# Expert 0 of a routed expert layer takes 64 token slots in place of 128, and the experts run in another order

## The chip, the cores and the metric

The kernel runs on one core of one Trainium2 chip. The metric is the device time of one execution in microseconds (us), as the median of the runs. TensorE (PE) multiplies matrices, VectorE (DVE) and ScalarE (ACT) do elementwise work, and the sequencer of SyncE (SP) issues all the loads of weights.

## The reference, cut to what matters

Layer 0 is a mixture of a state-space scan and retention with a dense feed-forward; layer 1 is differential attention with a routed expert layer behind it. The change touches only that last layer, which works on 256 tokens of width 1024:

```python
def moe(h, w_router, w_gate, w_up, w_down):
    logits = (h @ w_router).astype(jnp.float32)
    top_val, top_idx = lax.top_k(logits, TOP_K)          # 2 of 8
    top_w = jax.nn.softmax(top_val, axis=-1)
    combine = jnp.sum(jax.nn.one_hot(top_idx, N_EXPERTS, dtype=jnp.float32) * top_w[..., None], axis=-2)
    out = jnp.zeros_like(h)
    for e in range(N_EXPERTS):
        out = out + combine[..., e:e + 1].astype(h.dtype) * swiglu(h, w_gate[e], w_up[e], w_down[e])
    return out
```

`swiglu(h, g, u, d)` is `(silu(h @ g) * (h @ u)) @ d`, with 3584 hidden features in each expert, in 32-bit floats. The 256 tokens choose 512 experts in all, 64 for each expert in the mean. Worked out with the reference on its own inputs, experts 0 to 7 get 60, 52, 39, 90, 48, 47, 107 and 69 tokens.

## The kernel before, in words

Each expert's weights are read once, as 42 loads of two units of 128 x 1024 (1024 KB, here called a pair): 28 pairs of gate and up weights (`exp_gu`), then 14 of down weights (`exp_d`). A pair goes to half of a room named `wide`, or, two pairs in ten, to two tiles named `raw` of 512 KB each. Ten pairs find room at a time, besides five more that are loaded ahead of the layer into memory that the attention has left (`raw2`, L1380). A load waits in SP's queue until its room has been read; all loads stand in one queue in their order.

There are two ways to run an expert.

- Wide, 128 token slots (`expert`, L1480): each unit of weights is split by ACT (L183) and DVE (L184) into a high and a low part (`wsplit`), and each product is three matmuls of 512 columns (`mm3`, L194 to L196).
- Narrow, 64 token slots (`expert_half`, L1413): the weights are multiplied as they are, in 32-bit floats, with two products side by side in the two halves of the array (L1446 for gate and up, L1460 for down).

In both, the tokens of the next expert are gathered (`gather`, L1357 on PE) between the gate-up part and the down part, and the results are scattered back to the tokens at the end (L1525 and L1526, or L1473).

Expert 0 always is itself (`ORDER` starts with it, and its number is a constant), so that its weights can be loaded before the routing is known. The other seven places are filled by count: `sorted` ranks the experts, so place 1 holds the expert with most tokens, and place 7 that with fewest. The place's expert number is a value in memory, `self.ids`, which SP reads into a register (L1245, `TENSOR_LOAD`) before it can issue that place's loads. Places 0 to 3 are wide, places 4 to 7 narrow, in the order wide and narrow in turn: 0, 7, 1, 6, 2, 5, 3, 4. Below, W0 is the wide expert at place 0, N7 the narrow one at place 7, and so on.

If an expert has more tokens than slots, a general path behind the eight experts runs it again for the rest (L1251 to L1265). It is skipped when none has more. The Tile framework orders each engine's instructions by its own estimate; a block `issue_after(x)` makes its instructions stand behind `x` in their engine's queue, without a wait.

Of the kernel before, what the change touches and what calls it, by code (L numbers as in the profile page):

```python
# [19 lines left out]
P = 128  # L20
# [5 lines left out]
NE = 8  # L26
CAP = P
HALF = 64

ORDER = (0, 7, 1, 6, 2, 5, 3, 4)  # L30
SLOTS = (CAP,) * 4 + (HALF,) * 4
FE = 3584
LAM_INIT = 0.8 - 0.6 * math.exp(-0.3)

# [105 lines left out]
class Net:  # L140
# [18 lines left out]
    def mm(self, i):  # L159
        return self.pp.tile([P, 512], F32, name=f"mm{i}", tag=f"mm{i}", bufs=1)  # L160
# [12 lines left out]

    def wraw(self, ap):
        t = self.pw.tile([P, 1024], F32, name="raw", tag="raw", bufs=5)
        self.nc.sync.dma_start(t, ap)
        return t

    def wsplit(self, raw):
# [274 lines left out]
    def run(self):  # L454
        self.start()
        self.layer0()
        self.layer1()
        self.experts()
# [704 lines left out]
class Layer1Experts(Layer1):  # L1163
# [72 lines left out]
    def experts(self):  # L1236
        nc = self.nc
        v = nc.vector
        self.nraw, self.wide, self.al_slot, self.rest_slot = -5, (2, 3, 0, 1), 4, 4
        self.place, self.eid, self.rooms = self.rank, [0] * NE, {}  # L1240
        g = self.gather(0, 0)
        self.sorted()
        for i, n in enumerate(ORDER):
            if n:
                self.eid[n] = nc.values_load(self.ids[0:1, n:n + 1], engines=[mybir.EngineType.SP],  # L1245
                                             min_val=0, max_val=NE - 1)
            nxt = ORDER[i + 1] if i + 1 < NE else None
            run = self.expert if SLOTS[n] == CAP else self.expert_half
            g = run(n, g, 0, nxt, not i, nxt is None)

        more = nc.values_load(self.more[0:1, 0:1], min_val=0, max_val=256)  # L1251
        with self.tc.If(more > 0):
            self.nraw, self.wide, self.al_slot, self.rooms = 0, (3, 0, 1), 2, {}
            for t in range(2):
                v.memset(self.moe[:, t, :], 0.0)
            for n in range(NE):
                extra = nc.values_load(self.extra[0:1, n:n + 1], min_val=-P, max_val=256)
                with self.tc.If(extra > 0):
                    self.expert(n, self.gather(n, SLOTS[n]), SLOTS[n], None, False, False)
            for t in range(2):  # L1260
                for j in range(2):
                    c = slice(512 * j, 512 * j + 512)
                    u = self.scr("s3")
                    v.tensor_tensor(u, self.moe[:, t, c], self.rest[:, 2, c], op=ALU.mult)
                    self.put(t, c, u)  # L1265

    def sorted(self):

        nc = self.nc
        v = nc.vector  # L1270
        room = self.pc.tile([P, 384], F32, name="order", tag="dt_ex")
        at = [0]

        def new(shape):
            n = math.prod(shape)
            at[0] += n
            r = room[:, at[0] - n:at[0]]
            return r.rearrange("p (a b) -> p a b", b=shape[1]) if len(shape) == 2 else r

        e8 = lambda ap: ap[:, None, :].to_broadcast([P, NE, NE])  # L1280
        io = self.con[:, C_IO:C_IO + NE]
        pn = self.tr()
        for t in range(2):
            nc.tensor.matmul(pn[:, 0:NE], self.con[:, C_ONE:C_ONE + P], self.sel[:, t, :], start=t == 0, stop=t == 1)
        cnt, key, pos = (new([NE]) for _ in range(3))
        v.tensor_copy(cnt, pn[:, 0:NE])
        v.tensor_copy(key, pn[:, 0:NE])
        v.tensor_scalar(key[:, 0:1], key[:, 0:1], 1024.0, None, op0=ALU.add)
        cmp = self.scr("s3", (P, 2, NE, NE))
        mine, other = key[:, :, None].to_broadcast([P, NE, NE]), e8(key)  # L1290
        v.tensor_tensor(cmp[:, 0], other, mine, op=ALU.is_equal)
        v.tensor_tensor(cmp[:, 1], other, mine, op=ALU.is_gt)
        v.tensor_tensor(cmp[:, 0], cmp[:, 0], self.con[:, C_TIE:C_TIE + NE * NE].rearrange("p (a b) -> p a b", b=NE),
                        op=ALU.mult)
        v.tensor_reduce(pos, cmp.rearrange("p i a b -> p a i b"), axis=AX.XY, op=ALU.add)
        v.tensor_scalar(pos, pos, 1.0, None, op0=ALU.add)

        hot = new([NE, NE])
        v.tensor_tensor(hot, e8(pos), io[:, :, None].to_broadcast([P, NE, NE]), op=ALU.is_equal)
        self.place, self.wts = (new([2, NE]) for _ in range(2))  # L1300
        num = new([2, NE])
        u = self.scr("s3", (P, 2, NE, NE))
        for src, dst in ((self.rank, self.place), (self.cw, self.wts)):
            v.tensor_tensor(u, src[:, :, None, :].to_broadcast([P, 2, NE, NE]),
                            hot[:, None].to_broadcast([P, 2, NE, NE]), op=ALU.mult)
            v.tensor_reduce(dst, u, axis=AX.X, op=ALU.add)
        v.tensor_tensor(u[:, 0], e8(io), hot, op=ALU.mult)
        v.tensor_tensor(u[:, 1], e8(cnt), hot, op=ALU.mult)
        v.tensor_reduce(num, u, axis=AX.X, op=ALU.add)
        v.tensor_scalar(num[:, 0], num[:, 0], -1.0, None, op0=ALU.add)  # L1310
        self.ids = new([NE]).bitcast(I32)
        v.tensor_copy(self.ids, num[:, 0])
        for lo, hi, cap in ((0, 4, CAP), (4, NE, HALF)):
            v.tensor_scalar(num[:, 1, lo:hi], num[:, 1, lo:hi], -float(cap), None, op0=ALU.add)
        self.extra = new([NE]).bitcast(I32)
        v.tensor_copy(self.extra, num[:, 1])
        top = new([1])
        v.tensor_reduce(top, num[:, 1], axis=AX.X, op=ALU.max)
        v.tensor_scalar(top, top, 0.0, None, op0=ALU.max)
        self.more = new([1]).bitcast(I32)  # L1320
        v.tensor_copy(self.more, top)
# [7 lines left out]
    def gather(self, n, base):  # L1329
# [4 lines left out]
        v = nc.vector  # L1334
        half = SLOTS[n] == HALF and not base
        w = HALF if half else P
# [43 lines left out]
    def raw2(self, ap):  # L1380

        n = self.nraw
        self.nraw += 1

        k = n + 5 if n < 0 else n % (2 + 2 * len(self.wide)) - 2
        if n >= 0 and k < 0:
            return [self.wraw(ap[:, 1024 * i:1024 * i + 1024]) for i in range(2)]
        if n == -1:
            t = self.x[:, 0:2, :]
        else:  # L1390

            key = (k // 2, n < 0)
            if key not in self.rooms:
                self.rooms[key] = self.big(((5, 4) if n < 0 else self.wide)[k // 2], (P, 4, 1024), name="wide")
            t = self.rooms[key][:, 2 * (k % 2):2 * (k % 2) + 2]
        self.nc.sync.dma_start(t.rearrange("p u c -> p (u c)"), ap)
        return [t[:, i] for i in range(2)]

    def weights(self, name, n, *at):
# [13 lines left out]
    def expert_half(self, n, gathered, base, nxt, first, final):  # L1413

        nc = self.nc
        v = nc.vector
# [6 lines left out]
        ap = self.big(5, (P, FE // P, HALF), name="ef")  # L1423
# [7 lines left out]
        t = None  # L1431
        for b in range(FE // 512):
# [3 lines left out]
            for u in range(0, KD, 2):  # L1436
# [4 lines left out]
                for i in range(2):  # L1441
                    k = u + i
                    for g in range(2):
                        for h, s in enumerate(sides):
                            c = 512 * g + 256 * h
# [4 lines left out]
            t = self.scr("s3", (P, 256))  # L1450
# [18 lines left out]
        for t in range(2):  # L1469
            for j, s in enumerate(sides):  # L1470
                c = slice(512 * j, 512 * j + 512)
                pt = self.tr()
                mm(pt, pT[s, P * t:P * t + P], y[s], start=True, stop=True)  # L1473
                if final:
                    self.put(t, c, pt)
                else:
                    v.tensor_tensor(self.moe[:, t, c], self.moe[:, t, c], pt, op=ALU.add)
        return out

    def expert(self, n, gathered, base, nxt, first, final):  # L1480
# [27 lines left out]
        for u in range(0, nd, 2):  # L1508
            raw = self.raw2(self.weights("exp_d", n, u // 2))
            w = [self.wsplit(r) for r in raw]  # L1510
            steps = [(f, j) for f in (u, u + 1) for j in range(2)]
            for f, j in sorted(steps, key=lambda s: s[1]) if u == nd - 2 else steps:
                hi, lo = w[f - u]
                c = slice(512 * j, 512 * j + 512)
                self.mm3(py[j], ah[:, f, :], al[:, f, :], hi[:, c], lo[:, c], f == 0, f == nd - 1)
# [36 lines left out]
```

## Time and profile before

| | us |
|---|---|
| median of 3 runs | 2021.04 |
| lowest and highest run | 2015.29, 2026.21 |
| the profiled execution's own time | 2024.08 |
| span of its profile, first to last instruction | 2021.8 |
| PE busy in it | 1950.6 |

The span is 2.3 us shorter than its own execution. The expert layer takes the last 900 us of it. Times in the profile count from the start of the span.

### The profile page before, as it was taken

How to read it: one execution, taken by the hardware profiler on the slowest of the kernel's cores; microseconds unless marked ns; L12 is line 12 of the kernel's file. 1: busy time of each engine (PE TensorE's matmuls, PEld its weight loads, DVE VectorE, ACT ScalarE, POOL GpSimd, SP SyncE). 2: the span in 40 equal slices, each digit the busy share in tenths (PEclk: the TensorE clock that was granted, in tenths of full speed). 3: DMA queues.
4: the chain of work that ended last, by engine and by line, in shares of the span. 5: the costliest groups of instructions: out<-in, count | busy, mean ns of one | idle time of the engine just before them, and what ended most of it. 6: DMA issues, size and time to landing. Idle time of an engine off the chain costs nothing.

```text
span 2021.8 us, 26680 instructions
## 1 busy us (share of the span) xinstructions
PE 1950.6 (96%) x9894; PEld 1444.9 (71%) x9894; DVE 1226.4 (61%) x2105; ACT 906.1 (45%) x1373; POOL 10.1 (1%) x12
## 2 busy tenths in 40 slices
PE   7999999999999999999989999989999999999996
PEld 4776778777888888877857887648863786558762
DVE  5568578745877565577666886049811984059710
ACT  5535356533423212245365775138712773148610
POOL 0000000000000000000000000000000000000010
PEclk9999999999999999999999999999999999989999
DMA  8323434442655555424325499999999999999897
GB/s 319 114 94 105 145 112 150 136 141 64 207 181 174 174 174 167 155 94 116 114 105 219 166 344 337 418 418 417 369 390 418 417 379 362 417 418 390 341 376 312
DMA packets 103865, 502.68 MB, mean 249 GB/s; under 512 B 13104, under 2 KB 13744, under 8 KB 69296
## 3 DMA queue, kind: packets, MB, share of 16 engines
q1 hardware_dynamic: 103728, 500.91, 66.2%
q8 instruction: 79, 1.29, 0.3%
q14 instruction: 58, 0.48, 0.1%
HBM read 495.62 MB, written 5.24 MB: 248 GB/s over the span
## 4 chain that ended last, share of the span: by engine, by line
PE 81%; DMA 9%; DVE 6%; ACT 3%; issue 1%; SPq 0%; ACTq 0%; DVEq 0%
PE mm L196 17%; PE mm L195 17%; PE mm L194 17%; PE mm L1446 8%; DMA wide<-exp_d 3%; PE acc L195 2%; PE acc L196 2%; PE acc L194 2%; DMA wide<-exp_gu 2%; DVE lo L184 2%; DMA raw<-exp_d 2%; PE acc L1460 2%; PE tr L1357 1%; PE acc L315 1%; PE tr L1473 1%
## 5 line engine op out<-in xcount | busy, mean ns | idle before, releaser
L183 ACT ACTIVATE hi<-raw 128x1024 fp32r<-128x1024 f32 x224 | 237.3, 1060 | 411.5 <-PE mm L196 204.8
L184 DVE TENSOR_TENSOR lo<-raw,hi 128x1024 fp32r<-128x1024 f32 x224 | 273.0, 1222 | 177.1 <-ACT hi L183 169.9
L184 DVE TENSOR_TENSOR lo<-wide,hi 128x1024 fp32r<-128x1024 f32 x268 | 324.7, 1223 | 37.0 <-ACT hi L183 16.7
L183 ACT ACTIVATE hi<-wide 128x1024 fp32r<-128x1024 f32 x268 | 282.2, 1061 | 77.7 <-PE mm L196 52.2
L195 PE MATMUL mm<-lo,q 128*128 128x512 f32 x448 | 178.9, 399 | 2.1 <-DVE lo L184 2.0
L196 PE MATMUL mm<-hi,q 128*128 128x512 f32 x448 | 176.8, 395 | 0.0
L194 PE MATMUL mm<-hi,hh 128*128 128x512 f32 x416 | 169.0, 407 | 1.7 <-DVE b L856 1.3
L1446 PE MATMUL mm<-wide,q 128*64 128x256 f32 x1424 | 168.3, 382 | 0.0
L195 PE MATMUL mm<-lo,hh 128*128 128x512 f32 x416 | 165.2, 397 | 0.0
L196 PE MATMUL mm<-hi,hl 128*128 128x512 f32 x416 | 164.7, 398 | 0.0
L194 PE MATMUL mm<-hi,q 128*128 128x512 f32 x448 | 159.6, 397 | 0.0
L194 PE MATMUL mm<-h2h,hi 128*128 128x512 f32 (+1 forms) x376 | 142.5, 379 | 1.3 <-ACT hi L183 1.3
L195 PE MATMUL mm<-h2l,hi 128*128 128x512 f32 (+1 forms) x376 | 141.9, 377 | 0.0
L196 PE MATMUL mm<-h2h,lo 128*128 128x512 f32 (+1 forms) x376 | 141.7, 378 | 0.0
L1446 PEld LDWEIGHTS mm<-wide,q 128*64 128x64 f32 x1424 | 100.4, 137 | 55.8 <-issue 8.6
L1451 DVE TENSOR_TENSOR s<-s,mm 128x256 f32<-128x256 f32 x28 | 11.8, 421 | 192.7 <-ACT s L1449 192.7
L1460 PE MATMUL acc<-wide,ef 128*64 128x512 f32 x360 | 88.2, 601 | 18.6 <-DMA wide<-exp_d 18.6
L195 PEld LDWEIGHTS mm<-lo,q 128*128 128x128 f32 x448 | 85.4, 191 | 25.5 <-DVE lo L184 4.7
L194 PEld LDWEIGHTS mm<-hi,q 128*128 128x128 f32 x448 | 85.0, 190 | 22.8 <-ACT hi L183 3.0
L194 PEld LDWEIGHTS mm<-hi,hh 128*128 128x128 f32 x416 | 78.9, 190 | 27.9 <-issue 8.9
L196 PEld LDWEIGHTS mm<-hi,q 128*128 128x128 f32 x448 | 85.4, 191 | 18.5 <-issue 1.5
L196 PEld LDWEIGHTS mm<-hi,hl 128*128 128x128 f32 x416 | 78.7, 190 | 17.0 <-issue 0.8
(393 smaller groups left out, 3327.8 us busy)
## 6 DMA issues: line engine op xcount, KB each, us to landing
wide<-exp_gu SPq DMA_DIRECT2D x177, 1024.0 KB, 10.6
wide<-exp_d SPq DMA_DIRECT2D x91, 1024.0 KB, 11.8
raw<-exp_gu SPq DMA_DIRECT2D x92, 512.0 KB, 10.9
raw<-odd_wmod SPq DMA_DIRECT2D x48, 512.0 KB, 4.3
raw<-w_in SPq DMA_DIRECT2D x44, 512.0 KB, 3.7
raw<-ffn_gu SPq DMA_DIRECT2D x44, 512.0 KB, 4.4
raw<-exp_d SPq DMA_DIRECT2D x42, 512.0 KB, 15.0
raw<-even_wmod SPq DMA_DIRECT2D x36, 512.0 KB, 3.7
```

What stands on the lines that cost most here:

```text
L183: nc.scalar.activation(hi, raw, AF.Copy)
L184: nc.vector.tensor_tensor(lo, raw, hi.bitcast(F32), op=ALU.subtract)
L194: mm(ps, lh, rh, start=first, stop=False, skip_group_check=skip)
L195: mm(ps, lh, rl, start=False, stop=False, skip_group_check=skip)
L196: mm(ps, ll, rh, start=False, stop=last, skip_group_check=skip)
L315: nc.tensor.matmul(ps[r:r + 32, :], self.cond[:, k, :], raw[:, 512 * kk:512 * kk + 512], start=k < 4, stop=k >= 4)
L1357: nc.tensor.matmul(pt[:, w * kk:w * kk + w], self.x[:, 2 + t, P * (k + kk):P * (k + kk) + P], pn[:, t, 0:w], start=t == 0, stop=t == 1)
L1446: behind = mm(ps[s, 256 * g:256 * g + 256], xg[:, k, :], raw[i][:, c:c + 256], start=k + g == 0, stop=k == KD - 1, skip_group_check=True)
L1451: v.tensor_tensor(t, sg, ps[:, 256:512], op=ALU.mult)
L1460: mm(py[s], ap[:, f, :], raw[f - u][:, 512 * j:512 * j + 512], start=f == 0, stop=f == nd - 1, skip_group_check=True)
L1473: mm(pt, pT[s, P * t:P * t + P], y[s], start=True, stop=True)
```

## The change

Places 0 and 4 to 7 are narrow now, 1 to 3 wide. The order is 0, 1, 7, 2, 6, 3, 5, 4: N0, W1, N7, W2, N6, W3, N5, N4. The narrow function learns to write the sum of the outputs as the first expert. The general path gets a second pass for place 0, since expert 0 can have up to 256 tokens, and 64 + 128 don't hold them. SP's read of a place's expert number is placed behind the last load of the expert before it.

```diff
-ORDER = (0, 7, 1, 6, 2, 5, 3, 4)
-SLOTS = (CAP,) * 4 + (HALF,) * 4
+ORDER = (0, 1, 7, 2, 6, 3, 5, 4)
+SLOTS = (HALF,) + (CAP,) * 3 + (HALF,) * 4
...
     def wraw(self, ap):
         t = self.pw.tile([P, 1024], F32, name="raw", tag="raw", bufs=5)
-        self.nc.sync.dma_start(t, ap)
+        self.loaded = self.nc.sync.dma_start(t, ap)
         return t
...
             if n:
-                self.eid[n] = nc.values_load(self.ids[0:1, n:n + 1], engines=[mybir.EngineType.SP],
-                                             min_val=0, max_val=NE - 1)
+                with self.tc.issue_after(self.loaded.ins):
+                    self.eid[n] = nc.values_load(self.ids[0:1, n:n + 1], engines=[mybir.EngineType.SP],
+                                                 min_val=0, max_val=NE - 1)
...
                 with self.tc.If(extra > 0):
                     self.expert(n, self.gather(n, SLOTS[n]), SLOTS[n], None, False, False)
+                if not n:
+                    with self.tc.If(extra > P):
+                        self.expert(n, self.gather(n, SLOTS[n] + P), SLOTS[n] + P, None, False, False)
...
-        for lo, hi, cap in ((0, 4, CAP), (4, NE, HALF)):
+        for lo, hi, cap in ((0, 1, HALF), (1, 4, CAP), (4, NE, HALF)):
             v.tensor_scalar(num[:, 1, lo:hi], num[:, 1, lo:hi], -float(cap), None, op0=ALU.add)
...
-        self.nc.sync.dma_start(t.rearrange("p u c -> p (u c)"), ap)
+        self.loaded = self.nc.sync.dma_start(t.rearrange("p u c -> p (u c)"), ap)
...
                 if final:
                     self.put(t, c, pt)
+                elif first:
+                    v.tensor_copy(self.moe[:, t, c], pt)
                 else:
                     v.tensor_tensor(self.moe[:, t, c], self.moe[:, t, c], pt, op=ALU.add)
```

## Rows read from the trace of the kernel before

**Rows 1.** The page's second part: the span in 40 slices of 50.5 us; each digit is a busy share in tenths.

```profile
PE   7999999999999999999989999989999999999996
...
DMA  8323434442655555424325499999999999999897
```

**Rows 2.** The busy time of each engine in stretches of 50 us, in which W0 runs and ends, N7 runs and W1 begins. The columns are the stretch, its length, the busy us (and count) of PE, PEld, DVE, ACT and POOL, then the granted clock of TensorE (1.00 is 2.4 GHz, 0.50 is 1.2 GHz), the share of the DMA engines, and GB/s.

```profile
1100.00:1150.00 50.00, 46.90 (x236) 39.92 (x235) 41.01 (x109) 34.48 (x48) 0.00 (x0) 0.90 0.37 136
1150.00:1200.00 50.00, 50.00 (x229) 40.94 (x228) 46.90 (x44) 40.92 (x44) 0.00 (x0) 1.00 0.98 367
1200.00:1250.00 50.00, 50.00 (x246) 39.29 (x244) 38.57 (x37) 33.41 (x40) 0.00 (x0) 1.00 0.86 327
1250.00:1300.00 50.00, 50.00 (x435) 31.62 (x435) 3.98 (x9) 5.58 (x15) 0.00 (x0) 1.00 0.99 394
1300.00:1350.00 50.00, 44.11 (x199) 19.05 (x196) 11.82 (x16) 12.71 (x23) 0.00 (x0) 1.00 1.01 417
```

**Rows 3.** The timeline of PE where the experts meet: start, busy us, line, tile written and tiles read, count, and in brackets the idle time and who ended it. In order: the gather of W0's tokens and W0's first matmul; a narrow gather inside W0; the first matmul of N7; the first row and the last of N7's down part; the first matmul of N4 and the last row of its down part.

```profile
1113.47 6.05 PE L1357 MATMUL tr<-s,x 128*128 128x128 f32 x32
...
1120.38 0.50 PE L194 MATMUL mm<-hi,q 128*128 128x512 f32 x1
...
1204.02 3.68 PE L1357 MATMUL tr<-s,x 128*128 128x64 f32 x32
...
1245.38 0.65 PE L1446 MATMUL mm<-wide,q 128*64 128x256 f32 x2
...
1305.68 1.93 PE L1460 MATMUL acc<-wide,ef 128*64 128x512 f32 x6
...
1335.88 1.94 PE L1460 MATMUL acc<-wide,ef 128*64 128x512 f32 x8 [0.47 <-DMA wide<-exp_d]
...
1917.23 0.65 PE L1446 MATMUL mm<-wide,q 128*64 128x256 f32 x2
...
2008.83 1.92 PE L1460 MATMUL acc<-raw,ef 128*64 128x512 f32 x8
```

**Rows 4.** The same timeline inside N7: two pairs of its gate-up part with parts of the next gather between them, a stretch of its down part, and the first of seven gaps in a row that end with a load (the last of them is the row at 1335.88 in rows 3).

```profile
1298.52 1.95 PE L1446 MATMUL mm<-wide,q 128*64 128x256 f32 x16
1300.39 1.60 PE L1357 MATMUL tr<-s,x 128*128 128x128 f32 x12
1301.93 1.95 PE L1446 MATMUL mm<-wide,q 128*64 128x256 f32 x16
1303.81 1.38 PE L1357 MATMUL tr<-s,x 128*128 128x128 f32 x10
...
1307.91 7.51 PE L1460 MATMUL acc<-wide,ef 128*64 128x512 f32 x33
...
1320.91 1.94 PE L1460 MATMUL acc<-wide,ef 128*64 128x512 f32 x8 [1.40 <-DMA wide<-exp_d]
```

**Rows 5.** The timeline of SP's queue: all loads of expert weights up to the first that had to wait for W0 to read its room (`wide` and `x` 1024 KB each, `raw` 512 KB).

```profile
886.84 0.33 SPq L1396 DMA_DIRECT2D x<-exp_gu  x1
...
1014.27 0.80 SPq L1396 DMA_DIRECT2D wide<-exp_gu  x2
...
1018.67 64.14 SPq L1396 DMA_DIRECT2D wide<-exp_gu  x6
1085.03 7.13 SPq L176 DMA_DIRECT2D raw<-exp_gu  x3
1092.25 0.38 SPq L1396 DMA_DIRECT2D wide<-exp_gu  x1
1094.57 0.33 SPq L176 DMA_DIRECT2D raw<-exp_gu  x1
1094.95 0.42 SPq L1396 DMA_DIRECT2D wide<-exp_gu  x1
1097.29 0.33 SPq L176 DMA_DIRECT2D raw<-exp_gu  x1
1103.10 0.80 SPq L1396 DMA_DIRECT2D wide<-exp_gu  x2
1136.59 3.12 SPq L176 DMA_DIRECT2D raw<-exp_gu  x3
```

**Rows 6.** The DMA issues in the stretch 1000 to 1110 us: tile and source, count, KB each, median us from issue to landing.

```profile
raw<-exp_gu SPq DMA_DIRECT2D x5, 512.0 KB, 4.9
```

**Rows 7.** SP's reads of the expert numbers: SP's wait on the line that makes them (us in total, times, longest), and the read itself (shortest, median and longest ns, first and last start).

```profile
SPq L1245 <- DVE order L1312: 31.2, 1, 31.2
...
L1245 SPq TENSOR_LOAD <-order x7: 263/276/468, 1135.1 to 1889.1; - x7
```

**Rows 8.** DVE's timeline: the making of the numbers, and the first tile `raw` of W0 read for its low part.

```profile
1134.93 0.16 DVE L1312 CAST order<-order 128x8 int32<-128x8 f32 x1
1135.00 1.22 DVE L184 TENSOR_TENSOR lo<-raw,hi 128x1024 fp32r<-128x1024 f32 x1
```

**Rows 9.** Busy time by stretches of 20 us, columns as in rows 2: the end of N5, the change to W3, and a stretch of N4's down part.

```profile
1760.00:1780.00 20.00, 16.49 (x72) 5.22 (x70) 0.00 (x0) 0.00 (x0) 0.00 (x0) 1.00 1.02 419
1780.00:1800.00 20.00, 18.43 (x41) 9.36 (x38) 9.84 (x11) 8.10 (x9) 0.00 (x0) 0.66 1.02 416
1980.00:2000.00 20.00, 15.42 (x66) 3.75 (x64) 0.00 (x0) 0.00 (x0) 0.00 (x0) 1.00 1.02 420
```

## The prediction

> **What bounds the kernel now.** I read the page's slices first. PE is busy 9 tenths or more nearly everywhere, and from slice 24 on the DMA engines are too [rows 1]. So the expert layer has two limits close together, and a mean says nothing; I went by stretches. While W0 runs, the DMA share is 0.37, 0.98 and 0.86, and PE is busy 46.9, 50 and 50 of 50 us: W0 is bound by PE. While N7 runs PE is first full and then busy 44 of 50, with the DMA at 417 GB/s: N7 ends bound by its loads [rows 2]. PE's timeline shows that in single instructions: a pair of N7's gate-up part takes PE 1.87 us (1298.52 to 1300.39) [rows 4], and at the end of N7's down part each row waits for a load, from 1320.91 to 1335.88 six steps of 2.495 us [rows 3, 4]. So a pair costs 2.495 us by DMA and 1.87 us by PE in a narrow expert. A wide one can't be faster than its matmuls: W0 took 1245.4 - 1120.4 = 125.0 us for 42 pairs, 2.98 us each [rows 3].
>
> What the reader is to see: a wide expert is slower than its loads, a narrow one faster; a narrow one behind a wide one eats what the wide one's time let the DMA put aside, and then waits.
>
> **The change part by part.**
>
> *W0 becomes N0.* By SP's timeline 15.5 pairs are issued before W0's first matmul (1 + 2 + 6 + 1 + 1 + 2 pairs of `wide` and `x`, five `raw` of half a pair = 2.5) and then nothing until 1136.59 [rows 5], because all room is full. This store is the reason that place 0 can gain what the others can't: it needs only 26.5 of its 42 pairs from the DMA.
>
> N0's start: W0's gather took 6.05 us, a narrow one later took 3.68, at a full clock; W0's first matmul came 0.86 us behind its gather [rows 3]. Between 1113.5 + 3.7 + 0.9 = 1118.1 and 1120.4 I take 1119.6, since the clock in that stretch is below 1 [rows 2].
>
> N0 by PE: 28 pairs x 1.87 = 52.4, and the gather of W1 (12 + 10 of its 32 matmuls took 1.54 + 1.38 us, so 4.2) make 56.6 us [rows 4]. N7 needed 1305.68 - 1245.38 = 60.3 [rows 3], which holds W0's scatter too; N0 has none in front. I take 58. Down: 33 matmuls in 7.51 us, so 112 in 25.5 [rows 4]. End by PE: 1119.6 + 58 + 25.5 = 1203.
>
> N0 by DMA: the next load waits until N0 has read the first tile `raw`, that is five pairs and a half: 1119.6 + 5.5 x 1.87 + 0.4 to issue = 1130.3. The queue is empty then; a half pair landed 4.9 us after its issue [rows 6], of which 1.25 is its transfer, so 3.6 us are latency. 1130.3 + 3.6 + 26.5 x 2.495 = 1200, and 1.9 for the last pair: 1202. The two limits meet, so N0 ends at about 1203, and PE's own work before it doesn't change. W0 ended at 1245.4: **-42 us**. Bounds: 1200 (the DMA with the early start), and 1120.4 + 60.3 + 32.1 (N7's whole down part with its waits, 1305.68 to 1337.8) = 1213; so -45 to -32.
>
> *The six experts between* are N7, W1, N6, W2, N5, W3 before, from N7's first matmul at 1245.38 to N4's at 1917.23, 671.9 us [rows 3]. They are W1, N7, W2, N6, W3, N5 after it. Each wide one still follows a narrow one that ended out of loads, each narrow one a wide one: no change, **0**.
>
> *N4 follows N5 instead of W3.* Before it took 2010.75 - 1917.23 = 93.5 us [rows 3], less than its 42 x 2.495 = 104.8 us of loads, as W3 had let the DMA run ahead. Behind N5 nothing is put aside: 104.8 from N5's last load to its own. **+11**. Bounds: 0, if something is still in store, and a slower TensorE.
>
> That last bound is a matter of the clock. N5's end had PE busy 16.5 of 20 us and the clock at 1.00, N4's down part 15.4 of 20 and 1.00; but at the change from N5 to W3 the mean is 0.66 over 20 us, which is 13.6 us at the lower level, 1.2 GHz [rows 9]. The Trainium skill, "TensorE: Matmul & The Clock Gate", section "HAM oscillation — how this bites in real kernels", says that a matmul loop that waits for a load between bursts falls back to half the clock, again and again. By that rule N4, which will wait at each pair, would run its 60.3 + 25.5 us of PE work at half speed, 172 us, and the sum would be +36 instead of -31. The trace agrees for waits at the change of experts, and disagrees for the short waits of 0.5 us at each pair [rows 4, 9]; by the rows the sum stays.
>
> *The reads of the expert numbers.* SP's wait for them is 31.2 us [rows 7], the largest single thing that the edit to L1245 takes away. It is worth almost nothing in this trace. The numbers are made at 1134.93; the first `raw` that the next load needs is read by DVE at 1135.00 to 1136.22 [rows 8], and that load is issued at 1136.59 [rows 5]. SP stood behind a read, but the room wasn't free either: the cover is the full store. Without the edit the read would have gone bad here, as N0 frees the room at 1130. Now all seven reads stand between two experts' loads; behind each stand the next place's 42 loads, and PE waits for those. The read takes 0.28 us [rows 7], while a load keeps the DMA busy for 2.495 us with more in the queue: **0**; if that cover went, about 1 us each with its register work, 4 that move, so 4 us.
>
> *Small things.* Copying N0's sums instead of adding them and a third `tensor_scalar` in `sorted` lie on engines that are idle in a narrow expert (DVE 4.0, ACT 5.6 of 50 us [rows 2]): 0. What W0's DVE and ACT did (84 units split) is gone, and both were off the path. The second pass for place 0 is code in a skipped branch; expert 0 has 60 tokens, so it isn't run: 0, and at most 1 us for the jump.
>
> **Sum:** -42 + 0 + 11 + 0 = -31 us. The profiled execution took 2024.08 us (its span 2021.8 and 2.3 around it), so 1993; it lies 3 us above the median of the runs, and against the median it is 1990.
>
> **The rivals.**
>
> *More gain.* N4 pays nothing and the 13.6 us at the lower clock don't come back: -42 - 7 = -49 at most, or 1972 to 1980. For it: such a stretch belongs to one change of experts here, and nothing says that it must come again. Against: N4 needs all 42 pairs, and N5 waits for loads at its end [rows 9].
>
> *Less gain.* N0 goes at N7's pace, with waits in its down part, and ends at 1213: -32 + 11 = -21, and with one more stretch at the lower clock at N5's end -14: 2000 to 2010. For it: N0's two limits lie within 2 us of each other, and any waste shows. Against: the store of 15.5 pairs.
>
> *No change.* If the read in the queue held SP until the loads in flight had landed, each of the seven borders would cost a landing of 4.9 us, 34 in all, which eats the sum. For it: reads are now at every border. Against: the last read, at 1889.1 [rows 7], stood before N4's loads already, and a wait of SP's own shows on the first of them alone (31.2 us, once).
>
> *Slower.* N4 at the lower clock: a pair would take 3.74 us by PE, 1.25 more than its load. That takes the gain of 31 away after 25 of N4's pairs, 93 us at half clock; all of N4 gives 2057. For it: the 0.66 of rows 9, and the two levels differ by more than a narrow expert's slack (1.87 against 2.495 us). The Trainium skill's rule above speaks for it as well. Against: the clock stayed at 1.00 through two such stretches.
>
> *The change doesn't do what it says:* were expert 0 over 64 tokens, the general path would run a whole wide expert, 125 us more at least: 2115. Against: 60 tokens by the reference.
>
> **How the numbers follow.** The forecast (1980 to 2000) has 0.60, more gain 0.13, less gain 0.15; these three are faster by over 0.5% (about 10 us, which is what a measurement of this kernel can tell from no change): 0.88. No change 0.07. Slower 0.05, of which the lower clock has 0.03 and the general path 0.02. The time is the forecast's, 1990. The range goes from N0 at its best with a little of the extra gain, 1976, to the less gain's middle, 2005; what lies outside are the last two cases (0.12) and the ends of the gains.
>
> **What would show it.** Right: the first matmul of the wide expert's gate-up near 1205 instead of N7's at 1245; loads issued again at about 1130, with the DMA share near 1 from there to W1's end; 670 to 675 us from N0's end to N5's; each row of N4's gate-up part ending a wait for a load, 105 us in all. Wrong: N0's down part with gaps of 0.5 us from its start, SP's gaps of 5 us around the reads, N4 with a clock below 1, or any matmul behind L1259.

## The result, and the profile after

The changed kernel takes 1994.62 us (median; 1992.13 to 1999.70), the kernel before, run beside it, 2022.17 us. The ratio is 0.9884, with a 95% interval of 0.9858 to 0.9910: faster, by 27.6 us in the medians. The profiled execution took 1992.13 us with a span of 1990.0, 31.8 us under the span of before. One execution among all the runs below, of gather_128_fill, went at a mean clock of 0.556 (3203.83 us) and is left out of every comparison.

The page's second part after, as in [rows 1]:

```profile
PE   6999999999999999999999999999999999999986
...
PEclk9999999999999999999998799999999999999999
DMA  8332434442655455532433499999999999999997
```

Both limits are still close together. What has changed is where the DMA's full part begins, and the stretches of 50 us that answer to [rows 2] show it:

```profile
1100.00:1150.00 50.00, 48.50 (x331) 36.31 (x331) 16.26 (x86) 11.70 (x25) 0.00 (x0) 0.80 0.43 164
1150.00:1200.00 50.00, 50.00 (x362) 27.43 (x360) 3.46 (x8) 7.98 (x21) 0.00 (x0) 1.00 1.02 418
1200.00:1250.00 50.00, 47.38 (x197) 31.76 (x194) 35.58 (x35) 30.59 (x34) 0.00 (x0) 1.00 1.02 418
...
1300.00:1350.00 50.00, 49.64 (x249) 37.25 (x249) 34.13 (x34) 29.96 (x37) 0.00 (x0) 1.00 0.88 331
```

From 1150 to 1250 us the DMA share is 1.02 where it was 0.98 and 0.86, and ACT and DVE are nearly free while N0 runs (8.0 and 3.5 of 50 us). The dip of the DMA share that stood at W0's end (0.86) now stands at W1's end (0.88).

PE's timeline where the experts meet, as in [rows 3]: part of N0's gather, its first matmul, the first and last rows of its down part, the rest of N5's down part, and the last row of N4's.

```profile
1114.28 6.64 PE L1362 MATMUL tr<-s,x 128*128 128x64 f32 x30
...
1121.36 1.12 PE L1451 MATMUL mm<-wide,q 128*64 128x256 f32 x2
...
1181.96 1.93 PE L1465 MATMUL acc<-wide,ef 128*64 128x512 f32 x6
...
1206.97 1.94 PE L1465 MATMUL acc<-wide,ef 128*64 128x512 f32 x8 [0.45 <-DMA wide<-exp_d]
...
1871.57 1.46 PE L1465 MATMUL acc<-wide,ef 128*64 128x512 f32 x6
...
1977.07 1.92 PE L1465 MATMUL acc<-raw,ef 128*64 128x512 f32 x8
```

N0's matmuls end at 1208.9 us (W0's at 1245.2), N5's at 1873.0, N4's at 1979.0. So the first expert gives back 36.3 us, the six between take 664.1 in place of 672.1, and N4 takes 106.0 in place of 93.5: -36.3 - 8.0 + 12.5 = -31.8, which is the difference of the spans.

SP's timeline around the first load that has to wait for N0, as in [rows 5], and below it SP's own wait in that stretch, as in [rows 7]:

```profile
1103.32 0.80 SPq L1401 DMA_DIRECT2D wide<-exp_gu  x2
1135.39 3.45 SPq L176 DMA_DIRECT2D raw<-exp_gu  x4
```

```profile
SPq L1253 <- DVE order L1326: 24.6, 1, 24.6
SPq L176 <- PE mm L1451: 7.6, 4, 5.8
```

The reads of the expert numbers are gone from here, and the read of the branch's value (L1253) has slid into their place. It is over by 1129.5; the load comes 6 us later, and SP's wait on its line (L176, 5.8 us the longest) is for N0's matmuls, so again it is the room that is missing, not SP.

The reads themselves (shortest, median and longest ns, first and last start) now stand at the seven borders:

```profile
L1247 SPq TENSOR_LOAD <-order x7: 264/268/271, 1191.1 to 1852.9; - x7
```

None of them holds SP for the loads in flight. The last one starts at 1852.9, N4's first load goes out at 1853.7 (the chain below), and the load issued just before the read, the last of N5's, lands only at 1871.0.

The chain of work that ended last, from N4's loads on (start, length, what):

```profile
1853.72 19.84 DMA wide<-exp_gu
...
1873.68 15.47 DMA wide<-exp_gu
...
1954.54 20.65 DMA wide<-exp_d
...
1975.33 3.67 PE acc L1465 x16
```

Before, N4's chain began with 26 us of matmuls and reached the loads at 1943; now all of N4 is loads, down to its last two pairs.

### The profile page after: what moved, and what is told of

Read it like the earlier page. It is cut to its first block, busy times and chain, and to the rows that moved or that the text cites. A ratio compares the mean times of both kernels' runs of the same rounds, so it can differ in the third digit from the quotient of the medians.

```text
span 1990.0 us, 26467 instructions
## 1 busy us (share of the span) xinstructions
PE 1909.2 (96%) x9936; PEld 1385.0 (70%) x9936; DVE 1120.0 (56%) x2011; ACT 815.4 (41%) x1286; POOL 10.1 (1%) x12
## 4 chain that ended last, share of the span: by engine, by line
PE 74%; DMA 16%; DVE 6%; ACT 3%; issue 1%; SPq 0%; ACTq 0%; DVEq 0%
PE mm L195 16%; PE mm L196 16%; PE mm L194 16%; PE mm L1451 7%; DMA wide<-exp_d 5%; DMA wide<-exp_gu 5%; DMA raw<-exp_d 3%; PE acc L195 2%; PE acc L196 2%; PE acc L194 2%; DVE lo L184 1%; PE acc L315 1%; PE tr L1362 1%; PE acc L1465 1%; PE tr L1478 1%
## 5 line engine op out<-in xcount | busy, mean ns | idle before, releaser
L184 DVE TENSOR_TENSOR lo<-wide,hi 128x1024 fp32r<-128x1024 f32 x202 | 244.9, 1224 | 22.2 <-ACT hi L183 5.9
L183 ACT ACTIVATE hi<-wide 128x1024 fp32r<-128x1024 f32 x202 | 212.7, 1061 | 52.8 <-PE mm L196 34.0
L1451 PE MATMUL mm<-wide,q 128*64 128x256 f32 x1760 | 212.6, 386 | 8.5 <-DMA wide<-exp_gu 8.4
L1451 PEld LDWEIGHTS mm<-wide,q 128*64 128x64 f32 x1760 | 125.0, 138 | 82.8 <-DMA wide<-exp_gu 14.3
L195 PE MATMUL mm<-lo,q 128*128 128x512 f32 x336 | 133.0, 396 | 1.3 <-DVE lo L184 1.3
L196 PE MATMUL mm<-hi,q 128*128 128x512 f32 x336 | 131.3, 391 | 0.0
L1465 PE MATMUL acc<-wide,ef 128*64 128x512 f32 x456 | 111.7, 600 | 17.0 <-DMA wide<-exp_d 16.9
L194 PE MATMUL mm<-hi,q 128*128 128x512 f32 x336 | 112.9, 392 | 0.0
L194 PEld LDWEIGHTS mm<-hi,hh 128*128 128x128 f32 x416 | 78.2, 188 | 27.6 <-issue 9.7
L1465 PEld LDWEIGHTS acc<-wide,ef 128*64 128x64 f32 x456 | 32.8, 136 | 87.8 <-issue 52.2
L195 PEld LDWEIGHTS mm<-lo,hh 128*128 128x128 f32 x416 | 78.3, 188 | 17.0 <-issue 2.0
L341 DVE SCALAR_TENSOR_TENSOR s<-raw,cond,s 128x512 f32<-128x512 f32 x112 | 80.4, 749 | 1.2
```

What stands on the lines that cost most here:

```text
L183: nc.scalar.activation(hi, raw, AF.Copy)
L184: nc.vector.tensor_tensor(lo, raw, hi.bitcast(F32), op=ALU.subtract)
L194: mm(ps, lh, rh, start=first, stop=False, skip_group_check=skip)
L195: mm(ps, lh, rl, start=False, stop=False, skip_group_check=skip)
L196: mm(ps, ll, rh, start=False, stop=last, skip_group_check=skip)
L341: nc.vector.scalar_tensor_tensor(t, w, self.cond[:, k, i:i + 1], t, op0=ALU.mult, op1=ALU.add)
```

## The experiments

Stage ends read from each run's PE timeline, in us; a stage runs from the end of one expert's last down matmul to the end of the next one's, the first stage from its first matmul. The six are the experts between the first and N4. The fifth column adds up the stretches at 1.2 GHz inside the six, from the granted clock in each trace.

| kernel | first expert | the six | N4 | at 1.2 GHz in the six | span |
|---|---|---|---|---|---|
| before | 124.8 | 672.1 | 93.5 | 17.1 | 2021.8 |
| after | 87.6 | 664.1 | 106.0 | 0 | 1990.0 |
| after_again | 88.3 | 675.7 | 106.0 | 23.9 | 1998.8 |
| after_third | 87.9 | 670.1 | 106.0 | 13.7 | 1993.0 |
| gather_128 | 85.4 | 665.6 | 105.7 | 3.4 | 1984.3 |
| gather_128_again | 85.4 | 670.8 | 105.7 | 13.7 | 1986.6 |

**The changed kernel again: after_again.**

> The changed kernel once more, on the chip of the other three runs of this set, as their base. Every theory expects a ratio of 0.984 to 0.991 to the kernel before, N0's last down matmul near 1209 us, and TensorE's clock at 1.2 GHz from about 1107 to 1128 us.

Measured: ratio 0.9901 (0.9874 to 0.9929); N0's last down matmul ends at 1206.0, the clock is at the lower level from 1104.6 to 1125.0. Its span is 8.8 us longer than that of the first profile: the layer begins 3.6 us earlier (N0's first matmul at 1117.8, there at 1121.4), and the six take 11.6 us more. The stretches of 20 us at two changes from a narrow expert to a wide one show why:

```profile
1205.00:1225.00 20.00, 18.43 (x49) 9.90 (x46) 10.98 (x12) 9.07 (x10) 0.00 (x0) 0.74 1.02 417
1430.00:1450.00 20.00, 19.09 (x44) 9.59 (x41) 9.81 (x11) 7.28 (x9) 0.00 (x0) 0.66 1.02 419
```

In the table, against the first profile of after, 17.1 us at 1.2 GHz (before) go with 8.0 us more in the six, 23.9 (after_again) with 11.6 and 13.7 (after_third) with 6.0: a little under half a microsecond for each.

**The wider gather: gather_128.**

```diff
+        ww = w if n or base else P
...
-            nc.scalar.activation(pn[:, t, 0:w], p[:, t, 0:w], AF.Copy, scale=self.rs2[:, t:t + 1])
+            nc.scalar.activation(pn[:, t, 0:ww], p[:, t, 0:ww], AF.Copy, scale=self.rs2[:, t:t + 1])
...
-        per = 512 // w
+        per = 512 // ww
...
-                    nc.tensor.matmul(pt[:, w * kk:w * kk + w],
+                    nc.tensor.matmul(pt[:, ww * kk:ww * kk + ww],
```

> Only expert 0's gather is changed: its 32 matmuls stream 128 columns (the 64 wanted ones twice), as W0's gather did, and the second copy is not read. Theory (the clock): N0 came 6 us later than forecast because TensorE's clock rose at 1128.0 in place of 1118.0 us, and it rose late because the narrow gather keeps the array less busy than the wide one. Then the clock rises near 1118, the first load behind the store is issued near 1130 in place of 1135.4, N0's down part ends near 1203 in place of 1209, and the time is 4 to 6 us under that of the changed kernel. Rival (N0 is late because its gather starts late, behind the routing, and the clock is an effect of chance): the clock rises at 1124 or later, and the time is within 2 us of the changed kernel, or longer by the 2 us more that wide matmuls cost.

The clock is in the last column but two, over stretches of 4 us. First before, then after, then gather_128:

```profile
1116.00:1120.00 4.00, 3.80 (x26) 3.61 (x25) 1.23 (x3) 1.22 (x3) 0.00 (x0) 0.75 0.00 0
1120.00:1124.00 4.00, 4.00 (x24) 3.46 (x23) 2.59 (x10) 3.10 (x7) 0.00 (x0) 1.00 0.03 6
```

```profile
1120.00:1124.00 4.00, 3.89 (x17) 2.83 (x18) 1.35 (x7) 1.08 (x3) 0.00 (x0) 0.50 0.01 4
1124.00:1128.00 4.00, 4.00 (x22) 2.22 (x20) 3.76 (x22) 2.07 (x5) 0.00 (x0) 0.50 0.00 0
```

```profile
1112.00:1116.00 4.00, 4.00 (x24) 4.00 (x24) 0.50 (x2) 0.41 (x1) 0.00 (x0) 0.60 0.00 0
1116.00:1120.00 4.00, 4.00 (x33) 2.78 (x33) 1.43 (x7) 1.49 (x4) 0.00 (x0) 1.00 0.01 4
```

PE's timeline in gather_128 has the gather and N0's first matmul at

```profile
1111.63 5.06 PE L1363 MATMUL tr<-s,x 128*128 128x128 f32 x28 [1.01 <-ACT s L1355]
1116.62 0.65 PE L1452 MATMUL mm<-wide,q 128*64 128x256 f32 x2
```

and SP's the first load behind the store at

```profile
1128.34 3.45 SPq L176 DMA_DIRECT2D raw<-exp_gu  x4
```

In this run the layer began 2.7 us earlier than in after, so times are counted from the start of the gather's long row (1111.63, in after 1114.28). The clock fell at 1104.9 and rose 10.2 us later; in after it fell at 1107.6 and rose 20.5 us later. The load behind the store was issued 16.7 us behind the gather's start, in after 21.1; N0 ended 90.4 us behind it, at 1202.0, in after 94.6: 4.2 us less. Twice the columns cost next to nothing. In gather_128_again, where the clock rose only at the end of the gather, PE's timeline has it as

```profile
1107.60 6.32 PE L1363 MATMUL tr<-s,x 128*128 128x128 f32 x28 [1.01 <-ACT s L1355]
```

That is 0.226 us for each matmul, against 0.221 us for those of after.

The edit also lets the gathered tokens be copied out in two halves instead of all at once, which the theory doesn't name; but in after PE stood only 0.12 us ahead of N0's first matmul (1121.24 to 1121.36) and nowhere behind it until the waits for loads at N0's end, so that is not the 4 us. The theory stands on the place and the size in the profile. The median was 1987.42 us, 11.1 us under that of after_again; the profiles explain some 4 of them, so the pair was run again.

**The pair again: after_third and gather_128_again.**

> The changed kernel a third time, as the base of the next run. Both theories expect 1992 to 2000 us.

> The kernel with the wider gather again, beside the changed one, on one chip. In the first set it was 11 us faster by the medians, where the clock's earlier rise explains 5. Theory (5 us by the clock's rise; the rest was that the changed kernel had more stretches at 1.2 GHz later by chance): 4 to 7 us faster by the medians, and equal within 2 us where runs of equal mean clock less the first stretch are compared. Rival (the wider gather also keeps off later stretches): 9 to 12 us faster again.

Measured: 1993.40 us (ratio 0.9867) and 1992.66 us (0.9875, 0.9851 to 0.9900), no difference in the medians. The profiles repeat the first set: the clock rises 20.5 us and 10.2 us behind its fall, and N0 ends 95.0 and 91.6 us behind the start of the gather's long row, 3.4 us apart. Both profiles have 13.7 us at 1.2 GHz in the six, and their spans are 6.4 us apart (2.5 of it ahead of the gather); why the medians are not lies in the executions without a trace. Over the nine runs of either kernel in both sets the means are 1995.5 and 1990.6 us, 4.9 apart, with a standard error of some 2 us. Neither expectation is met as it was written. That the wider gather is worth about 4 us is shown by the profiles (all seven with the narrow gather end N0 94.4 to 95.3 us behind the gather's start, these two at 90.4 and 91.6), and not by the medians of these runs.

**More matmuls in PE's waits: gather_128_fill.**

```diff
+            if nxt is not None and SLOTS[nxt] == CAP and u >= nd // 2:
+                if u == nd // 2:
+                    fill = self.mm(3)
+                with self.tc.issue_after(behind.ins):
+                    for _ in range(1 if u < nd - 2 else 3):
+                        mm(fill[:, 0:P], self.ident, self.con[:, 0:P], start=True, stop=True)
```

> The kernel with the wider gather, and in each narrow expert that a wide one follows (N0, N7, N6) nine matmuls of 128 columns more on PE whose result nobody reads: one behind each of the last pairs of the down part, where PE waits for loads, and three behind the last, where it waits for ACT. Theory (the stretches at 1.2 GHz near these three changes, which come and go from run to run, follow PE's waits there): the profile shows no such stretch near the three changes, all runs have a mean clock of 0.988 or more, and the time is 0 to 4 us under the 1987.4 us of the wider gather alone, with less spread. Rival (the stretches don't hang on these waits, and the matmuls only stand in the way): stretches are still there, and the time is 0 to 4 us longer.

On PE's timeline the matmuls stand where they should, here behind N7; the stretch of 20 us at that change, below it, is at the full clock:

```profile
1423.90 1.94 PE L1466 MATMUL acc<-raw,ef 128*64 128x512 f32 x8
1425.77 0.94 PE L1473 MATMUL mm<-con 128*128 128x128 f32 x6
1426.64 1.12 PE L1485 MATMUL tr<-s,m 64*128 64x512 f32 x2
```

```profile
1425.00:1445.00 20.00, 19.87 (x76) 12.64 (x73) 15.68 (x17) 13.56 (x15) 0.00 (x0) 1.00 1.01 418
```

The profile has no lower stretch in the six, and the mean clock was 0.989 or more in the five runs compared. That fits the theory, but profiles without the extra matmuls can be free of such stretches too (the first of after is), so one profile can't show that the matmuls keep them off. The narrow experts that have them take up to 1.9 us longer (N0 87.3 in place of 85.4). The median is 1987.89 us (ratio 0.9851, 0.9817 to 0.9885), no better than gather_128's first 1987.42. Against all nine runs of the wider gather (1986.4 to 1997.7, mean 1990.6) the five here (1986.2 to 1990.0, mean 1987.8) are lower and closer together, but they are of another set. Whether the matmuls help stays open.

**The old order: order_old.** The changed kernel with `ORDER = (0, 7, 1, 6, 2, 5, 3, 4)`.

> The changed kernel, with the experts in the order of the kernel before: 0, 7, 1, 6, 2, 5, 3, 4, so that N7 stands behind N0 and N4 behind W3. Theory (two narrow experts in a row cost the second one its store, wherever they stand): N7 takes about 105 us from N0's end, N4 about 93, and the total is within 4 us of the changed kernel. Rival (only the last expert pays, because nothing follows that could use the time): N7 takes under 98 us, or the wide one behind it is shorter by as much, and the time is 8 to 12 us under that of the changed kernel.

PE's timeline: the end of N0, a pair of N7's gate-up part, N7's last row, N4's first matmul and its last row.

```profile
1201.84 1.94 PE L1465 MATMUL acc<-wide,ef 128*64 128x512 f32 x8 [0.47 <-DMA wide<-exp_d]
...
1226.90 1.95 PE L1451 MATMUL mm<-wide,q 128*64 128x256 f32 x16 [0.55 <-DMA wide<-exp_gu]
...
1307.75 1.94 PE L1465 MATMUL acc<-wide,ef 128*64 128x512 f32 x8 [0.47 <-DMA wide<-exp_d]
...
1885.83 0.65 PE L1451 MATMUL mm<-wide,q 128*64 128x256 f32 x2
...
1976.91 1.92 PE L1465 MATMUL acc<-raw,ef 128*64 128x512 f32 x8
```

N7, now behind N0, waits for loads from its gate-up part on and takes 105.9 us; N4, behind W3 again, takes 92.9. The median is 1998.68 us, 0.2 from after_again. So the price of two narrow experts in a row goes with the pair, not with the end of the kernel, and the new order alone shows no gain (the runs of order_old range from 1987 to 2011 us).

**Half of N4's loads: n4_half_loads.**

```diff
+        if lite:
+            self.loaded = self.nc.sync.dma_start(t[:, 0], ap[:, 0:1024])
+            return [t[:, 0]] * 2
...
-                raw = self.raw2(self.weights("exp_gu", n, b, u // 2))
+                raw = self.raw2(self.weights("exp_gu", n, b, u // 2), final)
```

> The changed kernel, in which the last expert, N4, loads only the first unit of each pair and uses it for both (so its part of the output is not the reference's). Theory (N4 behind N5 is bound by its loads at 2.5 us a pair): with half of them PE binds, 1.87 us a pair and 25 us for the down part, so N4 takes 84 to 90 us in place of 106 and the time is 16 to 22 us under that of the changed kernel. Rival (N4's last matmuls, or the sums on GpSimd and the output, set its end): within 5 us of the changed kernel.

```profile
1892.38 7.13 PE L1456 MATMUL mm<-wide,q 128*64 128x256 f32 x64
...
1942.55 13.89 PE L1470 MATMUL acc<-wide,ef 128*64 128x512 f32 x62
```

PE's timeline in N4 has four pairs of its gate-up part in 7.1 us, and no wait for a load: N4 takes 83.3 us, in place of 106.0, and the median is 1973.39 us (ratio 0.9775), 20 to 25 us under the three medians of the changed kernel. N4 is bound by its loads: they cost some 23 us over what PE needs.

**Eight narrow experts: all_narrow.** `SLOTS = (HALF,) * NE`, and the branch's value set to 0.

> The changed kernel with eight narrow experts and the general path switched off: the tokens beyond 64 of three experts are left out. Theory (a narrow expert behind a narrow one costs its loads, 42 x 2.495 = 104.8 us, and a wide one adds what its 130 us exceed that): N0 ends near 1209, seven times 105 us follow, the last down matmul ends near 1944 and the span is about 1955, 35 us under that of the changed kernel. Rival (TensorE's clock falls to half where every pair waits for its load): narrow experts of 130 us or more, and a time above that of the changed kernel.

Busy time by stretches of 100 us, columns as in [rows 2]:

```profile
1250.00:1350.00 100.00, 86.24 (x581) 41.63 (x578) 5.83 (x13) 8.62 (x24) 0.00 (x0) 1.00 1.02 417
...
1450.00:1550.00 100.00, 87.52 (x580) 42.53 (x576) 5.83 (x13) 9.00 (x25) 0.00 (x0) 0.98 1.02 417
```

Seven narrow experts in a row took 105.2 to 107.5 us each, 742.0 in all, with the DMA at 417 GB/s while their loads last; span 1957.9, median 1961.43 us. The clock stays up though PE waits at most pairs: two stretches of 3.4 us in 742. The rival of the clock falls here. The run also tells what the three wide experts still cost over the loads: 28 us (the same seven places take 664.1 + 106.0 = 770.1 us in after). The spans are 32.1 us apart because this run's layer also began 5.6 us earlier.

**The reads of the expert numbers: reads_free and before_reads_late.** The first is the changed kernel without `issue_after`, the second the kernel before with it and nothing else.

> The changed kernel without the order on SP's reads of the expert numbers: all seven, and the read of the branch's value that stands there in the changed kernel already, come before the first load that waits for room. Theory (reads cost about 1 us each, and are covered while the store is full): the eight reads end near 1136 us, where the changed kernel issues that load at 1135.4, so the load comes 1 to 2 us later and the time is 0 to 3 us longer. Rival (the order of the reads is a large part of the gain: 31.2 us of SP's waiting were taken away): 10 to 30 us longer than the changed kernel.

> The kernel before with one part of the change alone: SP's reads of the expert numbers stand behind the last load of the expert before. Theory (the 31.2 us that SP waited in the kernel before were covered by the full store): the first load behind the store is issued near 1136 us as before, W0 ends near 1245, and the time is within 4 us of the kernel before. Rival (that wait held back loads): the load is issued up to 30 us earlier, and the time is 10 us or more shorter.

For reads_free, SP's wait ahead of the first load behind the store, the reads, and SP's timeline at that load:

```profile
SPq L1246 <- DVE order L1322: 23.2, 1, 23.2
```

```profile
L1246 SPq TENSOR_LOAD <-order x7: 262/263/476, 1123.4 to 1127.1; - x7
```

```profile
1130.30 3.45 SPq L176 DMA_DIRECT2D raw<-exp_gu  x4
```

For before_reads_late, the wait, DVE's read of the first tile `raw`, and the load:

```profile
SPq L176 <- DVE order L1319: 32.4, 1, 32.4
```

```profile
1129.83 1.22 DVE L184 TENSOR_TENSOR lo<-raw,hi 128x1024 fp32r<-128x1024 f32 x1
...
1131.08 3.46 SPq L176 DMA_DIRECT2D raw<-exp_gu  x3
```

In reads_free the seven reads follow each other every 0.6 us and all are over by 1128.1, 2.2 us ahead of the load, which is issued 13.6 us behind N0's first matmul; in after it is 14.0. The median is 1992.62 us (ratio 0.9871, 0.9844 to 0.9897), 5.9 us under that of after_again, where up to 3 us more were expected; the two intervals overlap, and the rival's 10 to 30 us more did not come. In before_reads_late the 31.2 us have become 32.4 us, now on the load's own line. The instruction of DVE that the profile names starts as the read of the tile ends, at 1131.05, and the load goes out at 1131.08. So SP stands there just as long, for the room. The load comes 15.9 us behind W0's first matmul, 16.2 in [rows 3, 5]; the ratio is 1.0007 (0.9982 to 1.0032, that is 4 us less to 6 us more). No run shows a gain from the order of the reads in either kernel.

## Why the prediction was right

- *N0, forecast -42, measured -36.3.* The mechanism held: with 15.5 pairs in store, N0 ends where its PE work and its loads meet. The term was mis-sized by 5.7 us, in its first step, where I took N0's start at 1119.6 and counted its first 5.5 pairs at 1.87 us, the pace at the full clock. The start was chosen between a gather of 6.05 us (128 columns) and one of 3.68 (64 columns, at the full clock) [rows 3], but at the start of the layer the narrow gather took 6.64 us for 30 of its matmuls, no less than the wide one. The clock stayed at 1.2 GHz until 1128.0, N0 began at 1121.4 and read its first rooms at half pace, and the load that was to come at 1130.3 came at 1135.4. From there the sum holds: 1135.4 + 3.6 + 66.1 + 1.9 = 1207, measured 1208.9. The wider gather gave the clock and some 4 of the 5.7 us back.
- *The six experts between, forecast 0, measured -8.0.* By mechanism it was right: with the same clock their times are the same. The kernel before had 17.1 us at the lower level in them and after's first profile none. That is chance of the execution, as after_again (675.7) and after_third (670.1) show.
- *N4, forecast +11, measured +12.5.* Right in place, size and cause, and 105 to 108 us wherever a narrow expert with all its loads follows a narrow one (105.9 in order_old, 105.2 to 107.5 in all_narrow, 104.9 in gather_128_fill). The detail that each gate-up row of N4 would end a wait was wrong for the first ones: waits begin near 1897, since PE does N5's scatter among them (four rows of 1.12 us) and a few pairs come in meanwhile.
- *Luck in the sum.* Misses of +5.7, -8.0 and +1.5 us nearly cancel, and the spans differ by 31.8 us where the forecast had 31. The 8.0 are chance, so the mechanism alone gives -36.3 + 12.5 = -24; the medians, 27.6 us apart, are that and some of the same chance.
- *The reads, forecast 0, and up to 4.* 0 to the accuracy of two runs made for it. The wait of 31.2 us was covered by the full store. The aside that without the edit the reads would have gone bad, as N0 frees the room earlier, was wrong: N0 leaves DVE free, the numbers are made earlier too, and in reads_free the reads are over at 1128.1.
- *The rivals.* More gain had its second half (no lower stretch) in the one profile, and not N4's. No change fell in after: a read at a border took 0.27 us, with loads in flight. Less gain had N0's end near 1209 of its 1213, but by the clock at N0's start; N0 waited in its down part for its last two pairs alone. Slower, by the clock, fell with all_narrow: the lower clock that the Trainium skill, "TensorE: Matmul & The Clock Gate", section "HAM oscillation — how this bites in real kernels", ties to waits for loads didn't come at waits of about 0.5 us in 2.5; it came at some changes of experts. The loop of that section waits longer for a load than its matmuls take, which N4 does at no pair, so the rule was stretched in the prediction. No matmul of the general path ran.

## What to carry to other kernels

Where two limits alternate, cost a change by where each stage's store of loaded data begins and ends: work taken from the first stage, which starts with a full store, gains nearly all of it (36 us here), and the same work taken from a stage behind an equal one gains only what its loads allow (in all_narrow 28 us for three experts). A long wait in a queue's list is worth nothing while what stands behind it couldn't go either; look for the next thing that it needs. And where an edit changes the matmuls of a stage that begins at the low clock, don't take the clock's rise, or a time measured at the full clock, over from the old trace.

## What the runs showed of the hardware that was not expected

- At 1.2 GHz a matmul of the gather with 64 columns took as long as one with 128: 30 in 6.64 us in after, 28 in 6.32 us in gather_128_again, 0.22 us each. Yet TensorE's clock rose later behind the narrow ones: 20.5 us behind its fall in six of the seven profiles with the narrow gather there (17.1 in reads_free), 10.2 us in all five with 128 columns (before, before_reads_late, gather_128, gather_128_again, gather_128_fill). By the profile PE was busy in both; why it differs is not shown.
- Stretches of 3 to 14 us at 1.2 GHz come and go at the change from a narrow to a wide expert, from execution to execution of one program, and cost a little under half their length; PE's waits at such a change, behind the last down matmul, were of 0.8 us at most. They seem to be the larger part of what separates the single runs: in order_old 1987 us went with a mean clock of 0.990 and 2011 with 0.978, which is some 48 us more at 1.2 GHz and, at a little under half, an estimated 22 of the 24 us.
- The DMA engines moved 417 GB/s from 1150 to 1850 us in all_narrow, 2.5 us for each 1024 KB, with PE busy beside them.
